# Eighty-one groups of twelve equal matmuls behind the last product of a two-layer decoder

## The chip, the cores and the metric

The kernel runs on one core of one Trainium2 chip. The metric is the device time of one execution in microseconds (us), the median of the runs. The core's engines are TensorE (PE in the profile; its weight loads are shown apart as PEld), VectorE (DVE), ScalarE (ACT), GpSimd (POOL) and SyncE (SP, which issues transfers). They run side by side and wait for each other by semaphores. SBUF is the core's working memory with 128 partitions; PSUM is where TensorE writes its results, in banks of 512 four-byte columns.

## The reference

A decoder trunk of two layers on 512 tokens with 1024 features, all in four-byte floating point. Each layer does this:

```python
h = rmsnorm(x, g_mix)
z = h @ w_in
aq, ak, av, rq, rk, rv, rg, ga, gb = jnp.split(z, SPLIT_POINTS, axis=-1)
...
ya = sliding_window_sink_attention(aq, ak, av, sinks) @ w_a
...
r = chunkwise_retention(rq, rk, rv)
...
yb = r.astype(x.dtype) @ w_b
mixed = jax.nn.sigmoid(ga) * ya + jax.nn.sigmoid(gb) * yb
x = x + mixed @ w_out
h2 = rmsnorm(x, g_mlp)
x = x + jnp.square(jax.nn.relu(h2 @ w_up)) @ w_down
```

The output is the RMS norm of x after the second layer.

## The kernel before

**Precision.** TensorE multiplies in a reduced four-byte form, fp32r. To keep more of the precision, every operand is split into a high and a low part, both fp32r (`hi` and `lo` for weights, `xh` and `xl` for the scaled inputs, pairs of tiles `r` for intermediate results), and a product is made of three matmuls: high by high, high by low, low by high. The helper `products` (lines 390 to 397) issues them, and nearly all of the kernel's TensorE time stands on its three lines 395, 396 and 397.

**Operands of a matmul.** A matmul has a stationary operand of 128 columns, which a weight load (LDWEIGHTS) puts into the array, and a moving operand of up to 512 columns that streams past it. The result goes to PSUM. In a profile row `mm<-xh,hi 128*128 128x512` the first name behind the arrow is the moving operand, the second the stationary one, and 128x512 is the result, so 512 columns are moved. The program has one load for each matmul.

**Stages.** In each layer `layer_body` multiplies by the input projection chunk by chunk, with attention and retention worked in between, then by the value, mixing and output projections, then runs the feed-forward part in eight blocks of 512 hidden features (`pair` and `down`). Larger products use Strassen-like sums of quarters, with 256 columns moved at a time. Everywhere in these products both operands are read at unit step. Their starts are whole multiples of 128 elements from the tile's start, except that the weights of `pair` and of the output projection start 16 elements (`LINE`) further in.

**The end of the kernel.** The last block of the second layer is multiplied plainly by `down_plain`: eight results of 128 tokens by 512 features, each the sum of four times three matmuls with 512 columns. The last of them is made in two halves of 256 columns. Behind each, VectorE adds it to the residual, ScalarE sums the squares, and when a token block's second half is done the block is scaled by its inverse RMS (lines 1680 to 1685) and stored by two transfers (lines 1683 and 1686). TensorE has nothing to do after the last half.

**Order.** A scheduler sets the order of each engine's instructions from the code and from `tc.issue_after`, which keeps what is issued under it behind a given instruction. `latest[0]` holds the last product matmul issued. PSUM tiles come from two pools, `ps_mm` with five banks and `ps_aux` with three; a pool hands out its banks in turn, and who takes a bank waits until its earlier use is over.

**Tiles that the change reads.** `xh` and `xl` hold the scaled layer input, 128 partitions by eight chunks of 512 elements, 4096 elements in a row for each partition. They were last written ahead of the second layer's feed-forward part.

Of the kernel before, what the change touches and what calls it, by code (L numbers as in the profile page):

```python
# [17 lines left out]
P = 128  # L18
T = 512
# [26 lines left out]
N_PAIR = 14  # L46
UNIT = 1024
LINE = 16
ASIDE = ("pair", "wo")
WARM = 8  # L50
PACE = 0.8
# [61 lines left out]
def view(slot):  # L113
    return slot[0][:, slot[1], :]
# [3 lines left out]
def decoder(ctx, tc, xT, x_first, w_in, w_rv, w_a, w_b, w_wo, w_up, w_pair, w_down, w_end, tables, decay, band, g_last, out):  # L118
# [203 lines left out]
    def split_until(n):  # L322
        while state["split"] < min(n, len(order)):
# [7 lines left out]
            elif name == "block":  # L331
                add_block(i)
            raw = raws[i]
            aside = LINE if name in ASIDE else 0
            hi, lo = (
                wpool.tile([P, UNIT + 4 * LINE], F32R, tag=n, name=n, bufs=SPLIT + 1)[:, aside : aside + UNIT]
                for n in ("hi", "lo")
# [281 lines left out]
    def layer_body(layer):  # L619
# [759 lines left out]
        first_hi, first_lo = (view(t).rearrange("p (a t) -> p a t", t=H) for t in u_one)  # L1379
        columns = small.tile([P, 2 * NB + LINE], F32, tag="columns", name="columns", bufs=1)  # L1380
        factor, negative = (columns[:, i * NB : (i + 1) * NB] for i in range(2))
# [399 lines left out]
        layer_body(layer)  # L1781

def _by_chunk(w, cols):

    return w[:, cols].reshape(-1, P, len(cols)).transpose(1, 0, 2)
# [158 lines left out]
```

## Time and profile before

| what | value |
|---|---|
| time, median of 2 runs | 1454.8 us (1454.45 to 1455.14) |
| the profiled execution's own time | 1457.31 us |
| its span, first to last instruction | 1455.2 us |
| mean granted TensorE clock | 0.999 of full speed |
| matmuls and weight loads | 8041 and 8041 |

The span is that of the profiled execution. The profile gives the busy time of each engine, and for matmuls that needs care: they are pipelined, so that the next one starts long before the former has ended, and the ends are modelled. What a matmul costs in a stream is the distance from its start to the next one's start, which the timeline shows.

### The profile page before, as it was taken

The page shows a single profiled execution, that of the slowest core. Times are in us where ns is not written, and L with a number is a line of the kernel's source. Part 1 is how long each engine was busy: PE and PEld are TensorE (multiplying, and loading weights), DVE is VectorE, ACT ScalarE, POOL GpSimd, SP SyncE. Part 2 cuts the span into 40 slices and gives each one's busy share as a digit, 9 for nine tenths or more (in the row PEclk, how much of TensorE's full clock was granted, in tenths as well). Part 3 has the DMA queues.
Part 4 walks back from the last instruction along what each step waited for, and adds up shares of the span by engine and source line. Part 5 has one row for each costly group of instructions (what it writes and reads, how often), then busy time and mean ns, then how long its engine had stood idle before and what let it go on. Part 6 is the DMA issues. An engine that isn't in the chain of part 4 may idle for free.

```text
span 1455.2 us, 22150 instructions
## 1 busy us (share of the span) xinstructions
PE 1443.0 (99%) x8041; PEld 1258.8 (87%) x8041; DVE 1167.0 (80%) x1762; ACT 969.2 (67%) x1592; POOL 222.6 (15%) x329
## 2 busy tenths in 40 slices
PE   9999999999999999999999999999999999999998
PEld 7888888888988999999888888888889799999997
DVE  6978876866998888888778788687778988787885
ACT  6657555543687777777756575565437877777775
POOL 0011012112101111112201110112120011111120
PEclk9999999999999999999999999999999999999999
DMA  7598359799745677666955983797875477777664
GB/s 258 177 290 225 105 165 303 237 247 248 232 124 196 191 200 186 175 182 179 310 177 170 295 222 108 215 293 223 221 214 175 138 202 199 195 193 197 177 188 149
DMA packets 96428, 297.57 MB, mean 204 GB/s; under 512 B 11328, under 2 KB 11456, under 8 KB 90432
## 3 DMA queue, kind: packets, MB, share of 16 engines
q0 software_dynamic: 35936, 125.58, 37.2%
q1 hardware_dynamic: 59664, 169.27, 33.5%
q8 instruction: 63, 1.03, 0.3%
q10 hardware_dynamic: 720, 1.31, 0.2%
q14 instruction: 45, 0.37, 0.1%
HBM read 256.54 MB, written 115.87 MB: 256 GB/s over the span
## 4 chain that ended last, share of the span: by engine, by line
PE 94%; DMA 2%; ACT 2%; DVE 1%; issue 1%; SPq 0%; DVEq 0%; ACTq 0%
PE mm L395 23%; PE mm L396 23%; PE mm L397 22%; PE wo L1301 5%; PE b L395 2%; PE b L396 2%; PE b L397 2%; PE rv L396 2%; PE rv L395 2%; PE rv L397 2%; PE mm L410 2%; DMA raw<-w_pair_in 1%; PE score L778 1%; PE pT L743 1%; PE r L397 1%; PE r L396 1%
## 5 line engine op out<-in xcount | busy, mean ns | idle before, releaser
L343 ACT ACTIVATE hi<-raw 128x1024 fp32r<-128x1024 f32 (+1 forms) x387 | 394.3, 1021 | 257.5 <-PE mm L396 137.1
L344 DVE TENSOR_TENSOR lo<-raw,hi 128x1024 fp32r<-128x1024 f32 (+1 forms) x388 | 452.3, 1173 | 105.8 <-ACT hi L343 104.4
L395 PE MATMUL mm<-xh,hi 128*128 128x512 f32 (+1 forms) x976 | 343.1, 355 | 1.6 <-ACT xh L418 0.9
L396 PE MATMUL mm<-xl,hi 128*128 128x512 f32 (+1 forms) x976 | 343.6, 355 | 0.0
L397 PE MATMUL mm<-xh,lo 128*128 128x512 f32 (+1 forms) x976 | 339.5, 354 | 0.0
L395 PEld LDWEIGHTS mm<-xh,hi 128*128 128x128 f32 x976 | 183.9, 189 | 27.6 <-ACT xh L418 1.6
L396 PEld LDWEIGHTS mm<-xl,hi 128*128 128x128 f32 x976 | 185.0, 190 | 24.2
L397 PEld LDWEIGHTS mm<-xh,lo 128*128 128x128 f32 x976 | 182.7, 188 | 23.6
L397 PE MATMUL mm<-r,lo 128*128 128x256 f32 (+1 forms) x608 | 187.9, 309 | 0.0
L396 PE MATMUL mm<-r,hi 128*128 128x256 f32 (+1 forms) x608 | 187.9, 309 | 0.0
L395 PE MATMUL mm<-r,hi 128*128 128x256 f32 (+1 forms) x608 | 185.6, 309 | 0.5 <-ACT mm L1476 0.5
L395 PEld LDWEIGHTS mm<-r,hi 128*128 128x128 f32 x608 | 114.7, 189 | 8.5 <-ACT mm L1476 0.7
L396 PEld LDWEIGHTS mm<-r,hi 128*128 128x128 f32 x608 | 115.2, 189 | 7.8
L397 PEld LDWEIGHTS mm<-r,lo 128*128 128x128 f32 x608 | 114.1, 188 | 6.2
L1624 POOL DMA_DIRECT2D y<-eu x56 | 62.3, 1351 | 370.8 <-DVE eu L1609 370.2
L396 PE MATMUL mm<-lo,r 128*128 128x512 f32 (+1 forms) x276 | 104.6, 388 | 0.0
L397 PE MATMUL mm<-hi,r 128*128 128x512 f32 (+1 forms) x276 | 101.3, 387 | 0.0
L395 PE MATMUL mm<-hi,r 128*128 128x512 f32 (+1 forms) x276 | 98.4, 390 | 0.9 <-ACT eu L1619 0.6
L395 PE MATMUL b<-hi,r 128*128 128x512 f32 x180 | 70.5, 392 | 1.6 <-DVE eu L1609 1.2
L396 PE MATMUL b<-lo,r 128*128 128x512 f32 x180 | 70.3, 390 | 0.0
L1301 PE MATMUL wo<-r,hi 128*128 128x256 f32 x384 | 68.0, 281 | 0.0
L397 PE MATMUL b<-hi,r 128*128 128x512 f32 x180 | 67.9, 390 | 0.0
(323 smaller groups left out, 2679.5 us busy)
## 6 DMA issues: line engine op xcount, KB each, us to landing
raw<-w_in_in SPq DMA_DIRECT2D x73, 512.0 KB, 5.9
sums_down<-w_down_in POOLq DMA_DIRECT2D x30, 1024.0 KB, 11.6
sums_up<-w_pair_in POOLq DMA_DIRECT2D x56, 512.0 KB, 10.5
raw<-w_down_in SPq DMA_DIRECT2D x45, 512.0 KB, 7.8
raw<-w_pair_in SPq DMA_DIRECT2D x84, 256.0 KB, 3.7
y<-y POOLq DMA_DIRECT2D x63, 256.0 KB, 9.2
y<-eu POOLq DMA_DIRECT2D x61, 256.0 KB, 8.0
raw<-sums_down SPq DMA_DIRECT2D x30, 512.0 KB, 7.3
```

Source lines behind the costliest of these rows:

```text
L343: state["high"] = nc.scalar.activation(hi[:, at], raw[:, at], AF.Copy).ins
L344: nc.vector.tensor_tensor(lo[:, at], raw[:, at], f32(hi[:, at]), ALU.subtract)
L395: nc.tensor.matmul(ps, ah, bh, start=start and i == 0, stop=False, **more)
L396: nc.tensor.matmul(ps, ah, bl, start=False, stop=False, **more)
L397: latest[0] = nc.tensor.matmul(ps, al, bh, start=False, stop=stop and i == n - 1, **more).ins
L410: latest[0] = nc.tensor.matmul(ps, w[:, cols(j, c)], moving[k][low], start=first, stop=bool(final)).ins
L743: nc.tensor.transpose(pt[:, i * P : (i + 1) * P], sm[:, at : at + P], ident)
L778: nc.tensor.matmul(ps[:, g * w : (g + 1) * w], q_s[g][:, c, at], part[:, keys], start=i == 0, stop=i == 1)
L1301: latest[0] = nc.tensor.matmul(o, w[:, cols], v, start=start and first and n % 2 == 0 and w is hi and v is vh, stop=final and w is lo, ski ...
L1624: nc.gpsimd.dma_start(y[:, 2 * j + m, i * T : (i + 1) * T], t, **how)
```

## The change

A function `paces` is called once behind the two layers. It takes `xh` as a long row `mv` of 4096 elements for the moving operand and `xl` as a row `st` for the stationary one. Its inner `run` takes a bank of `ps_aux` and issues the same matmul twelve times into it, under `issue_after(latest[0])`. Each is complete in itself (`start` and `stop`), and nothing reads the result. The calls differ in width (512 or 256 columns) and in where the operands lie:

- the stationary operand at unit step, from 0, 8, ..., 120 elements on, and from 2, 4 and 12;
- the moving operand from 4 and 8 elements on;
- the stationary operand with a step of 2, 4, 8, 16 or 30 elements, from 0 and 16 on;
- the moving operand in pieces of 16 elements out of every 32, with the stationary operand at step 1, 8 or 16;
- the moving operand with a step of 2;
- the moving operand and the result both backwards, with the stationary operand from 0, 16, 32 and 48 on.

```diff
+REPEAT = 12
...
+    def paces():
+        mv, st = (t.rearrange("p k t -> p (k t)") for t in (xh, xl))
+
+        def run(n, a, b, backwards=False):
+            ps = bank(ps_aux, "pace")
+            o = ps[:, n - 1 :: -1] if backwards else ps[:, :n]
+            with tc.issue_after(latest[0]):
+                for _ in range(REPEAT):
+                    latest[0] = nc.tensor.matmul(o, a, b, start=True, stop=True).ins
+
+        def lines(at, n):
+            return mv[:, at : at + 2 * n].rearrange("p (a b) -> p a b", b=2 * LINE)[:, :, :LINE]
+
+        def spread(at, step):
+            return st[:, at : at + P * step : step] if step > 1 else st[:, at : at + P]
+
+        for at in range(0, P, 8):
+            for n in (T, P * 2):
+                run(n, spread(at, 1), mv[:, :n])
+        for at in (2, 4, 12):
+            run(T, spread(at, 1), mv[:, :T])
+        for at in (4, 8):
+            for back in (0, 16):
+                run(T, spread(back, 1), mv[:, at : at + T])
+        for step in (2, 4, 8, 16, 30):
+            for at in (0, 16):
+                for n in (T, P * 2):
+                    run(n, spread(at, step), mv[:, :n])
+        for step in (1, 8, 16):
+            for at in (0, 16):
+                for n in (T, P * 2):
+                    run(n, spread(at, step), lines(0, n))
+        for n in (T, P * 2):
+            run(n, spread(0, 1), mv[:, : 2 * n : 2])
+        for at in (0, 16, 32, 48):
+            for n in (T, P * 2):
+                run(n, spread(at, 1), mv[:, n - 1 :: -1], True)
+
+    paces()
```

Since the new constant stands at the file's head, the lines of the kernel are numbered one higher behind it (395 is 396 after the change). On TensorE the program before ends with the last half of the last product; `hi` is the moving weight tile, `r_85` the stationary one.

```order
L397 MATMUL mm<-hi,r_85 128x256
L395 MATMUL mm<-hi,r_85 128x256
L396 MATMUL mm<-lo,r_85 128x256
L397 MATMUL mm<-hi,r_85 128x256
L1941 UNCONDITIONAL_BRANCH
```

After the change the same place on TensorE reads as follows, with the waits in brackets; `PE_49` is TensorE's own count of finished work.

```order
L398 MATMUL mm<-hi,r_85 128x256
L1793 MATMUL pace<-xh,xl 128x512 x12
L1793 MATMUL pace<-xh,xl 128x256 x12
L1793 MATMUL pace<-xh,xl 128x512 x12
L1793 MATMUL pace<-xh,xl 128x256 [waits PE_49]
L1793 MATMUL pace<-xh,xl 128x256 x11
L1793 MATMUL pace<-xh,xl 128x512 [waits PE_49]
```

The groups stand behind everything else on TensorE, in the order of the code, and from the fourth on the first matmul of a group waits for the group that had the same bank. The rows of all other engines are the same as before.

## The prediction

> **What bounds the kernel now.** I read the page's busy shares first, then its chain of work, because the added work stands on one engine and the question is whether that engine sets the end.
>
> ```profile
> span 1455.2 us, 22150 instructions
> ...
> PE 1443.0 (99%) x8041; PEld 1258.8 (87%) x8041; DVE 1167.0 (80%) x1762; ACT 969.2 (67%) x1592; POOL 222.6 (15%) x329
> ...
> PEclk9999999999999999999999999999999999999999
> ...
> PE 94%; DMA 2%; ACT 2%; DVE 1%; issue 1%; SPq 0%; DVEq 0%; ACTq 0%
> ```
>
> TensorE (PE) has a matmul running in 99% of the span, 94% of the chain that ended last is PE, and the granted clock is full in every slice. PE and PEld have the same count, 8041: each matmul has a weight load of its own. So whatever is added to PE costs its full time, except where PE has already stopped. That exception is the tail, read from the timeline.
>
> ```profile
> 1434.99 0.40 PE L395 MATMUL mm<-hi,r 128*128 128x512 f32 x1
> ...
> 1445.66 0.39 PE L397 MATMUL mm<-hi,r 128*128 128x512 f32 x1
> 1445.88 0.28 PE L395 MATMUL mm<-hi,r 128*128 128x256 f32 x1
> ...
> 1448.52 0.28 PE L396 MATMUL mm<-lo,r 128*128 128x256 f32 x1
> 1448.64 0.28 PE L397 MATMUL mm<-hi,r 128*128 128x256 f32 x1
> ...
> 1450.61 0.72 ACT L1685 ACTIVATE x<-x,sq 128x512 f32<-128x512 f32 x1 [0.23 <-DVE sq L1681]
> ...
> 1451.36 0.37 ACTq L1686 DMA_DIRECT2D y_out<-x  x1
> ```
>
> The first column is the start. PE starts its last matmul at 1448.64. What follows is the last block's normalization on VectorE (DVE) and ScalarE (ACT) and its store, and the span ends at 1455.2, 6.5 us after PE's next free place (1448.64 + 0.12 = 1448.76). That is all the cover that the added matmuls can have.
>
> **The price of one added matmul.** The durations are of no use here, since matmuls overlap: what a stream costs is the distance from start to start. Between 1434.99 and 1445.88 stand 48 matmuls with 512 columns: 10.89 / 48 = 0.227 us each. From 1445.88 to 1448.64 are 23 steps of matmuls with 256 columns: 2.76 / 23 = 0.120 each. Two longer or odder stretches bound the second figure.
>
> ```profile
> 1379.83 0.28 PE L397 MATMUL mm<-r,lo 128*128 128x256 f32 x1
> ...
> 1384.43 0.28 PE L397 MATMUL mm<-xh,lo 128*128 128x256 f32 x1
> ...
> 1385.13 0.28 PE L396 MATMUL mm<-r,hi 128*128 128x256 f32 x1
> ...
> 1386.27 0.28 PE L397 MATMUL mm<-r,lo 128*128 128x256 f32 x1
> ```
>
> The first pair is 39 steps in 4.60 us, 0.118 each; the second 10 steps in 1.14, 0.114 each. I take 0.118, the longest stretch, with 0.114 and 0.120 as its ends.
>
> [...]
>
> What does a weight load cost by itself? Where matmuls are one column wide, the loads are all that is left.
>
> ```profile
> 24.96 0.95 PE L566 MATMUL ssq<-ones,acc 128*128 128x1 f32 x8
> 25.77 0.72 PE L397 MATMUL mm<-xh,lo 128*128 128x512 f32 x2
> ...
> L395 PEld LDWEIGHTS mm<-xh,hi 128*128 128x128 f32 x976 | 183.9, 189 | 27.6 <-ACT xh L418 1.6 <-DVE rot L640 1.1 <-ACT eu L1478 0.5
> ```
>
> Eight such matmuls take 25.77 - 24.96 = 0.81 us; the first load was done ahead, so seven loads take at most 0.81 / 7 = 0.115 each. The load's own row shows 0.189 us, but most of that lies beside the matmul ahead of it. So with 256 columns a step is 0.118 and the load nearly fills it (0.115); with 512 there is about 0.11 of slack. A slower load shows at once in the groups with 256 columns, and in those with 512 only when it about doubles.
>
> **The change, part by part.** Counting the calls gives 81 groups: 32 in the first loop, 3, 4, 20 with a stepped stationary operand, 12 with a moving operand in pieces, 2 with a moving step of two, 8 backwards. 44 have 512 columns and 37 have 256: 44 x 12 = 528 and 37 x 12 = 444, together 972 matmuls with 972 loads.
>
> - At the pace of the rows: 528 x 0.227 = 119.9 us and 444 x 0.118 = 52.4 us, 172.3 in all.
> - Stationary places of 0 to 120 elements and moving places of 4 and 8, at unit step (39 groups): nothing but the place is new, and the kernel's own matmuls already differ in place (weights 16 elements in, in the pair loop, against none elsewhere); the spread that these show is 0.114 to 0.120. I add nothing.
> - Stepped stationary operands, 28 groups (20 and 8 of the 12 in pieces), 14 of each width: no row shows one. From below a load in steps costs nothing more, since the load's 128 elements are the same number. From above, none of a load lies beside a matmul: 0.189 more for each of 336, 63.5 us. I take nothing, the value of the nearest row, a load of the same size at unit step.
> - Moving operand in pieces of 16 out of 32 elements, in steps of two, or backwards with the result also backwards (22 groups): no row shows these either. From below nothing; from above each column takes twice as long, as the 4-byte transposes show.
>
> ```profile
> 83.28 0.60 PE L743 MATMUL pT<-ident,sm 128*128 128x128 f32 x4
> ```
>
>   Four transposes of 128 columns: (0.60 - 0.27) / 3 = 0.11 us each, 0.86 ns a column, where the difference of the two widths, (0.227 - 0.118) / 256, is 0.43 ns. For 22 groups, 11 of each width, that is 132 x (0.227 + 0.118) = 45.5 us. I take nothing: the count of columns is unchanged, which is what the matmul rows scale with.
> - Waits: from the fourth group on, the first matmul of a group waits for PE's own count, that the group three earlier is done (three banks). Two groups of twelve lie between, at least 24 x 0.114 = 2.7 us, so the count is long there when it is asked for. The table of PE's waits bears it out: its longest row is 1.2 us, and none names PE itself, though products in it already wait that way. Behind a waiting matmul only later groups are queued. Cost: nothing; if it were not hidden, a drain of 0.28 at 78 groups is 22 us, inside the range.
> - Other engines: nothing is added or moved. The operands xh and xl were written long before and nothing is read from the results.
>
> ```profile
> PE b L395 <- DVE eu L1609: 1.2, 1, 1.2
> ...
> PE wo L1301 <- ACT xh L418: 0.2, 1, 0.2
> ...
> DMA to landing us min/median/max: 2.0/2.4/2.8
> ```
>
> The end: the last store is issued at 1451.36 and lands 2.0 to 2.8 later, so closing the program takes 1.0 to 1.8 us of the span (1455.2 less 1454.2 or 1453.4); I take 1.2. Now the close waits for PE. The first added matmul starts at 1448.76, the last at 1448.76 + 172.3 - 0.1 = 1621.0, it ends 0.28 later, and with 1.2 the span is 1622.4, that is 167.2 more than 1455.2. The whole tail of 1448.76 to 1455.2 disappears under the new stream. The profiled execution took 1457.31 us, 2.5 above the median of 1454.8, so for itself it would come to 1624.5; on the median it is 1454.8 + 167.2 = 1622.
>
> **The rivals.**
>
> - Half-pace loads. A load whose elements lie 16 bytes or more apart takes twice as long, 0.23 us. Steps of 4, 8, 16 and 30 elements are in 12 groups of each width: 144 x (0.230 - 0.118) + 144 x (0.230 - 0.227) = 16.6 us, giving 1639. For it speaks how tight the load is at 256 columns; against it, that no row shows any load slower than another in SBUF. [...]
> - Loads far slower, or stealing from the moving stream in both widths: half to all of the 63.5 us above, 1654 to 1686. That each load already costs its matmul something (0.118 for 256 columns at 0.43 ns is 0.008 above 0.110) speaks for some of it.
> - Backwards or stepped moving operands at half pace: the 8 backward groups and the 2 with step two are 60 x (0.227 + 0.118) = 20.7 us, giving 1643; the two alone, 4.1.
> - Loads that cost nothing, since the same weights are loaded twelve times: 0.43 ns a column gives 0.218 and, at the load's floor, 0.113: 528 x 0.218 + 444 x 0.113 = 165.3, giving 1615. [...]
> - Not slower by 2%: equal matmuls in a row are folded into one. 81 x 0.18 = 14.6 us, less the cover of 6.5, is 8 more: 1463. It decides from a stream below 6.5 + 29 us on. Against it: the warm-up at line 375 issues eight equal matmuls and the trace has all eight, with their loads.
>
> ```profile
> L375 PE MATMUL warm<-ones 128*128 128x512 f32 x8 | 3.8, 649 | 1.1 <-DVE ones L370 1.1
> L375 PEld LDWEIGHTS warm<-ones 128*128 128x128 f32 x8 | 2.5, 325 | 1.6 <-DVE ones L370 1.1
> ```
>
> **How the numbers follow.** Pace as in the rows, 1616 to 1628 around 1622: 0.40. Half-pace loads, around 1639: 0.26. Backward or stepped moving, 1626 to 1645: 0.12. Far slower loads, 1654 and more: 0.15. Free loads, 1615: 0.04. Folded: 0.02. A remainder of 0.01 that no case gives. The range of 1612 to 1660 takes in the first three and the free loads, 0.82, and cuts most of the slow loads. A measurement of this kernel tells about 2%, 29 us, from no change: slower 0.97, within 2% 0.02, faster 0.01.
>
> **What would show it.** In the profile after: 972 more on PE and on PEld, at line 1793, starting at about 1448.8; each group's twelve starts 0.227 or 0.114 to 0.120 apart; no row of waits of PE on PE; the granted clock still full; ScalarE's and VectorE's last work still ending near 1451.4. Half-pace loads would show as groups with steps of 4 and more and 256 columns near 0.23, with step 2 and the 512 ones unchanged. Slower moving operands would show in the last ten groups at both widths. The prediction is wrong if the stepped, cut or backward groups, 42 of the 81, run at a pace of their own; the 39 at unit step are its safe part.

## The result and the profile after

The changed kernel takes 1646.82 us, the median of 2 runs (1646.69 to 1646.94), against 1454.8 us (1454.45 to 1455.14) before: a ratio of 1.132, 95% interval 1.1271 to 1.1369. That is slower by 192.0 us. The forecast was 1622.0 with a range of 1612 to 1660, so the sign and the range held, and the centre lies 24.8 us too low.

These are the lines of after that answer to those shown of before: span, busy time of the engines, granted clock, and the chain that ended last by engine; the last row is from the view of that chain in order of time.

```profile
span 1644.7 us, 24094 instructions
...
PE 1637.6 (100%) x9013; PEld 1435.6 (87%) x9013; DVE 1167.4 (71%) x1762; ACT 968.6 (59%) x1592; POOL 223.0 (14%) x329
...
PEclk9999999999999999999999999999999999999999
...
PE 96%; ACT 2%; DMA 1%; DVE 1%; issue 0%; SPq 0%; DVEq 0%; ACTq 0%
...
1446.33 197.41 PE pace L1793 x972
```

9013 - 8041 = 972 matmuls and as many loads: all were issued and all were run, none folded into another. The other engines' busy times are those of before to within 0.6 us, and the clock stayed full in every slice. The last row (start, length, what it is) is the end of the chain of work: the added stream alone fills 197.41 us with nothing else in it, and only the 1.0 us of closing the program follows. The table of PE's waits has no row in which PE waits for PE.

So the stream itself was longer than the 172.3 us forecast, and the question is which groups. The next view gives the stream by stretches of time, each cut a little inside its first and last group. Its columns are the stretch and its length, the busy time and number of matmuls (PE) and of loads (PEld), the granted clock, the share of DMA, and GB/s.

```profile
1446.40:1532.60 86.20, 86.20 (x467) 74.16 (x466) 1.00 0.02 7
1533.10:1541.10 8.00, 8.00 (x46) 7.10 (x45) 1.00 0.00 0
1541.60:1586.90 45.30, 45.30 (x192) 45.30 (x191) 1.00 0.00 1
1587.40:1595.60 8.20, 8.20 (x47) 6.98 (x46) 1.00 0.00 0
1596.10:1618.20 22.10, 22.10 (x96) 22.10 (x95) 1.00 0.00 1
1618.70:1626.40 7.70, 7.70 (x24) 4.59 (x23) 1.00 0.00 0
1626.90:1643.40 16.50, 16.50 (x95) 14.34 (x94) 1.00 0.00 1
```

In the order of the code these are: unit places, stationary step 2, stationary steps 4 to 30, moving pieces with a unit stationary operand, the same with a stepped one, moving step two, and backwards. PEld gives a first hint. In five stretches loads are busy for 60% to 90% of the time; in the third and the fifth they are busy for all of it (45.30 of 45.30, 22.10 of 22.10). That alone proves little, since plain groups with 256 columns also keep the loads busy throughout (1.30 of 1.30 us in the second group). But plain groups with 512 columns don't (2.07 of 2.50 in the first), and here those do too, which points at the loads. The sixth is the opposite: 24 matmuls fill 7.70 us while their loads take only 4.59, which points at the moving operand.

Taken from the first matmul of each stretch to the first of the next, and set against the forecast's prices of 0.227 and 0.118 us:

| stretch | matmuls | us | forecast | more |
|---|---|---|---|---|
| unit places | 468 | 86.74 | 85.3 | 1.4 |
| stationary step 2 | 48 | 8.43 | 8.28 | 0.15 |
| stationary steps 4, 8, 16, 30 | 192 | 45.78 | 33.1 | 12.7 |
| moving pieces, unit stationary | 48 | 8.70 | 8.28 | 0.4 |
| moving pieces, stationary step 8 or 16 | 96 | 22.58 | 16.56 | 6.0 |
| moving step two | 24 | 8.22 | 4.14 | 4.1 |
| backwards | 96 | 16.96 | 16.56 | 0.4 |

Together 25.2 us: 18.7 from the two stretches with stationary steps of 4 and more, 4.1 from the moving step of two, 2.4 from all else. Within the third stretch, the groups with 256 columns run at 0.233 (step 4), 0.240 to 0.243 (step 8), 0.221 to 0.223 (step 16) and 0.243 to 0.244 us (step 30) from start to start, where the forecast had 0.118; those with 512 columns at 0.235 to 0.248. (This leaves out each group's first step, where it meets the group ahead: about 0.35 with 512 columns and 0.12 with 256, together two loads at this pace.) In the sixth, the widths take 0.455 and 0.230, twice the forecast.

The rest of the account is small. The products ended 2.6 us earlier in this execution than in the one of before (first added matmul at 1446.17, forecast 1448.76), and the program closed 1.25 us after the last matmul's start where 0.28 + 1.2 was forecast. 167.2 + 25.2 - 2.6 - 0.2 = 189.6, and the spans differ by 1644.7 - 1455.2 = 189.5.

### The profile page after: what moved, and what is told of

It is laid out like the page before. It is cut to its first block, busy times and chain, and to the rows that moved or that the text cites. A ratio compares the mean times of both kernels' runs of the same rounds, so it can differ in the third digit from the quotient of the medians.

```text
span 1644.7 us, 24094 instructions
## 1 busy us (share of the span) xinstructions
PE 1637.6 (100%) x9013; PEld 1435.6 (87%) x9013; DVE 1167.4 (71%) x1762; ACT 968.6 (59%) x1592; POOL 223.0 (14%) x329
## 4 chain that ended last, share of the span: by engine, by line
PE 96%; ACT 2%; DMA 1%; DVE 1%; issue 0%; SPq 0%; DVEq 0%; ACTq 0%
PE mm L396 20%; PE mm L398 20%; PE mm L397 20%; PE pace L1793 12%; PE wo L1302 5%; PE b L396 2%; PE b L397 2%; PE b L398 2%; PE rv L398 2%; PE rv L397 2%; PE rv L396 2%; PE mm L411 1%; PE score L779 1%; PE pT L744 1%; PE r L398 1%; PE r L397 1%
## 5 line engine op out<-in xcount | busy, mean ns | idle before, releaser
L1793 PE MATMUL pace<-xh,xl 128*128 128x512 f32 (+1 forms) x972 | 197.6, 366 | 0.0
L1793 PEld LDWEIGHTS pace<-xh,xl 128*128 128x128 f32 x972 | 177.7, 229 | 19.8 <-issue 3.0
L396 PE MATMUL b<-hi,r 128*128 128x512 f32 x180 | 70.5, 393 | 1.6 <-DVE eu L1610 1.2
```

The source lines that it names most:

```text
L396: nc.tensor.matmul(ps, ah, bh, start=start and i == 0, stop=False, **more)
L1793: latest[0] = nc.tensor.matmul(o, a, b, start=True, stop=True).ins
```

## The experiments

All but the last keep the changed kernel up to its last product and replace only what `paces` issues there, so the output is computed as before; the added results are unread in all of them. From the second experiment on a measured group has twenty-four matmuls, so that the distance from one row to the next, divided by 24, is the pace; "steady" leaves out a group's first steps. The paces in the five experiments with such groups come from one execution each. The plain group with 512 columns, which three of them have, came out at a steady 0.2272 each time.

### Steps of four and more, and the moving step of two, back at unit step

```diff
-        for step in (2, 4, 8, 16, 30):
+        for step in (2, 1, 1, 1, 1):
...
-        for step in (1, 8, 16):
+        for step in (1, 1, 1):
...
-            run(n, spread(0, 1), mv[:, : 2 * n : 2])
+            run(n, spread(0, 1), mv[:, :n])
```

> The changed kernel with 26 of its 81 groups put back to unit step: the 24 whose stationary operand has a step of 4, 8, 16 or 30, and the 2 whose moving operand has a step of 2. The 972 matmuls stay. Theory A (a step that leaves fewer than two of the read elements on a 16-byte line halves a weight load, and a step of two halves the moving stream; all else runs at the pace of unit step): in the changed kernel the 24 groups took 45.8 + 22.6 us and the 2 took 8.2; at unit step they should take 144 x (0.233 + 0.119) = 50.7 and 12 x (0.228 + 0.119) = 4.2, so 21.7 us less, 1625 against 1646.8. Theory B (the excess over 172 us belongs to the backward groups, the waits for a bank, or the end of the program): at most 10 us less, 1637 or more.

Measured: 1625.9 us (1624.45 to 1628.56), a ratio to before of 1.117, interval 1.1151 to 1.1188. Its page begins:

```profile
span 1622.4 us, 24094 instructions
...
PE 1615.7 (100%) x9013; PEld 1409.3 (87%) x9013; DVE 1167.7 (72%) x1762; ACT 969.5 (60%) x1592; POOL 223.1 (14%) x329
```

The same number of instructions, and the span is 22.3 us shorter than with the change as it is. Group by group, the 26 that were made plain take 54.8 us here and 76.6 in the changed kernel: 21.8 less, where theory A expected 21.7. (It is 12.39 in the stationary steps with a plain moving operand, 5.33 in those with a moving operand in pieces and 4.05 in the moving step of two.) The step of the operands is therefore the cause, and not the place in the program or the number of matmuls. The stationary step of 2, the moving pieces and the backward groups stayed as they were. What remains, 1625.9, is within 4 us of the forecast, which had taken steps to be free.

### What a stepped load costs

Twelve groups with a moving operand at unit step, 256 columns wide and then 32, and stationary steps of 1 to 31; `same` repeats one column 128 times.

```diff
+        run("one", P * 2, every(st, P, 1), half)
+        run("two", P * 2, every(st, P, 2), half)
+        run("three", P * 2, every(st, P, 3), half)
+        run("four", P * 2, every(st, P, 4), half)
...
+        run("oneslim", 32, every(st, P, 1), slim)
...
+        run("fourslim", 32, every(st, P, 4), slim)
+        run("sameslim", 32, same(st, P), slim)
```

> In place of the 81 groups, 12 groups of 24 with other steps of the stationary operand: 7 beside 256 moving columns, 5 beside 32, where only the load is left. Theory A (the load's read costs about 1.75 ns for each 16-byte line that it touches, and never less than 0.112 us): step 1, 2 and one column repeated 0.112 to 0.120 us a matmul; step 3 touches 96 lines, 0.17; steps 4, 5 and 31 touch 128 lines each, all 0.22 to 0.24. Beside 32 columns: 0.112, 0.112, 0.17, 0.225 for steps 1, 2, 3, 4 and 0.11 for the repeated column. Theory B (the distance to the element before decides: under 16 bytes free, from 16 on double): step 3 (12 bytes) stays at 0.118, 4, 5 and 31 as in A. Theory C (the step lengthens the load through conflicts with the moving stream alone): beside 32 columns step 4 stays near 0.12.

The timeline of PE, with one row for each group (start, length, instruction, number):

```profile
1448.65 3.04 PE L1792 MATMUL one<-xh,xl 128*128 128x256 f32 x24
1451.52 3.04 PE L1792 MATMUL two<-xh,xl 128*128 128x256 f32 x24
1454.40 4.32 PE L1792 MATMUL three<-xh,xl 128*128 128x256 f32 x24
1458.56 5.76 PE L1792 MATMUL four<-xh,xl 128*128 128x256 f32 x24
1464.16 5.65 PE L1792 MATMUL five<-xh,xl 128*128 128x256 f32 x24
...
1478.06 2.75 PE L1792 MATMUL oneslim<-xh,xl 128*128 128x32 f32 x24
1480.65 5.13 PE L1792 MATMUL twoslim<-xh,xl 128*128 128x32 f32 x24
...
1490.74 5.74 PE L1792 MATMUL fourslim<-xh,xl 128*128 128x32 f32 x24
1496.33 5.28 PE L1792 MATMUL sameslim<-xh,xl 128*128 128x32 f32 x24
```

Step 1 and step 2 run at 2.87 / 24 = 0.120, step 3 at 4.16 / 24 = 0.173, step 4 at 5.60 / 24 = 0.233, and steps 5 and 31 at 0.229 and 0.233. This is not a jump at a distance of 16 bytes, which would have left step 3 with its 12 bytes free. The price goes with a count: in groups of four elements from the tile's start, 16 bytes each and called lines here, the 128 elements touch 64 at step 2, 96 at step 3 and 128 from step 4 on, and 0.173 / 96 and 0.233 / 128 are both 1.8 ns a line. Among loads of 128 lines the price still varies: in the changed kernel from 0.221 at step 16 to 0.244 at step 30, or 1.7 to 1.9 ns a line, and no run shows why. At step 2 the 64 lines (0.116 at that price) just disappear behind what a load takes anyhow: with 32 columns and step 1, where the moving operand is out of the way, a steady step is 0.112.

Put by elements: with two to a line a matmul beside 256 columns takes no longer than with four (0.120 at steps 1 and 2), and with one it takes 1.94 times as long (0.233 against 0.120).

The slim groups hold a trap, which the granted clock shows (the columns now have DVE, ACT and POOL behind PEld, none busy; the clock stands third from the end).

```profile
1478.06:1480.65 2.59, 2.59 (x26) 2.59 (x25) 0.00 (x0) 0.00 (x0) 0.00 (x0) 1.00 0.03 6
1490.74:1496.30 5.56, 5.56 (x25) 5.56 (x26) 0.00 (x0) 0.00 (x0) 0.00 (x0) 0.50 0.00 0
```

From the group `twoslim` on the clock is 0.50, and `twoslim`'s steady 0.213 is the floor of a load at half clock and not the price of a step of 2: the repeated column, a single line, takes 0.213 as well. Yet `fourslim` is at 0.233 as `four` was at full clock. So the price of 128 lines doesn't scale with TensorE's clock. It is no conflict with the moving operand either, since with 32 columns there is next to none.

### What a stepped moving operand costs

Twelve groups with 512 columns and a stationary operand at unit step: moving steps of 1 to 7, pieces of two or four elements out of eight at two starts, and one column repeated.

```diff
+        run("two", T, plain, every(mv, T, 2))
+        run("three", T, plain, every(mv, T, 3))
...
+        run("pairs", T, plain, pieces(mv, T, 2, 8))
...
+        run("quads", T, plain, pieces(mv, T, 4, 8))
+        run("quadsacross", T, plain, pieces(mv, T, 4, 8, 2))
+        run("samecolumn", T, plain, same(mv, T))
...
+        run("weightsame", T, same(st, P), every(mv, T, 1))
```

> In place of the 81 groups, 12 groups of 24 with 512 moving columns in other patterns. Theory A (the moving read costs about 1.7 ns for each change of 16-byte line): unit step 128 lines, 0.227 us; step 2, 256 lines, 0.45; step 3, 384 lines, 0.67; steps 4 and 7, 512 lines, 0.88 to 0.92; pairs of every eight elements that share a line, 256 lines, 0.45; the same pairs three elements further on, so that each lies across two lines, 512 lines, 0.9; quads of every eight on one line 0.23, two elements further on 0.45; one column repeated 0.216 or less. Theory B (any step but one halves the rate, whatever the lines): steps 2, 3, 4 and 7 all 0.45, pairs and quads between 0.23 and 0.45 and the same wherever they start. [...]

The same view of this kernel:

```profile
1447.95 5.63 PE L1792 MATMUL one<-xh,xl 128*128 128x512 f32 x24
1453.41 11.04 PE L1792 MATMUL two<-xh,xl 128*128 128x512 f32 x24
1464.27 10.98 PE L1792 MATMUL three<-xh,xl 128*128 128x512 f32 x24
1475.07 11.26 PE L1792 MATMUL four<-xh,xl 128*128 128x512 f32 x24
1486.14 10.69 PE L1792 MATMUL seven<-xh,xl 128*128 128x512 f32 x24
1496.65 11.27 PE L1792 MATMUL pairs<-xh,xl 128*128 128x512 f32 x24
1507.74 11.22 PE L1792 MATMUL pairsacross<-xh,xl 128*128 128x512 f32 x24
1518.78 5.73 PE L1792 MATMUL quads<-xh,xl 128*128 128x512 f32 x24
1524.34 11.09 PE L1792 MATMUL quadsacross<-xh,xl 128*128 128x512 f32 x24
1535.26 5.43 PE L1792 MATMUL samecolumn<-xh,xl 128*128 128x512 f32 x24
1540.52 5.41 PE L1792 MATMUL bothsame<-xh,xl 128*128 128x512 f32 x24
```

Step 2 takes 0.453 and steps 3, 4 and 7 take 0.450, 0.461 and 0.438: the price doubles at once and then grows no more, about 0.88 ns a column. Four elements together run at full pace (0.231) when they fill one line and at half (0.455) when they start two elements further on and lie over two lines; pairs are at half pace whether both elements lie on one line (0.462) or on two (0.460). Both theories fell. The one that let the price grow with every further line was wrong from step 3 on and for the pairs on two lines, and the other was wrong on the groups of four.

Two elements to a line, at which a load costs no more (0.120), are not enough for the moving operand: at full clock two are half pace (0.453 at step 2), and full pace was seen only with four (0.231).

The last groups bear on a side question, why a plain matmul takes 0.227 and not 512 x 0.43 = 0.218. With one moving column repeated it takes 0.219 (5.26 / 24), with one weight column repeated 0.232: about 8 ns of the 0.227 go with reading different moving columns, and reading different weight columns adds nothing. Each matmul here still has its load, so whether a load beside the stream matters is not shown.

### The law on other shapes

Thirteen groups to try one formula: a moving operand takes 1.75 ns or more for each line that it touches, never less than 0.43 nor more than 0.88 ns a column; a load takes 1.75 or more for each line, never less than 0.112.

```diff
+        run("byone", T, plain, every(mv, T, 1, 1))
...
+        run("sixofeight", 3 * P, plain, pieces(mv, 3 * P, 6, 8))
+        run("sixteens", T, plain, pieces(mv, T, 16, 32))
+        run("sixteensbytwo", T, plain, pieces(mv, T, 16, 32, 2))
+        run("eightsbytwo", T, plain, pieces(mv, T, 8, 16, 2))
+        run("halvestwo", P * 2, plain, every(mv, P * 2, 2))
...
+        run("quarterthree", P, every(st, P, 3), mv[:, :P])
```

> In place of the 81 groups, 13 groups of 24. Nine with other moving patterns, four with a load of step 1 to 4 beside 128 moving columns, in place of the 32 beside which the clock fell to half. Moving: the runs so far give 0.43 ns a column where four neighbours share a 16-byte line and 0.88 where not, however far apart. Theory A (each line takes at least 1.75 ns and each column at most 0.88): unit step started one, two or three elements in costs a line more, 0.227 to 0.235; six of every eight elements, 384 columns, 0.225; pieces of sixteen 0.24 where they start on a line and 160 lines, 0.28, where they start two elements in; pieces of eight two elements in, 192 lines, 0.34; 256 columns at step 2, 0.225. Theory B (the whole instruction falls to 0.88 ns a column as soon as any group of four is not on one line): 0.45 for unit step started one, two or three in, 0.34 for six of eight, 0.45 for pieces started two in. Loads beside 128 columns: if the full clock holds, 0.112, 0.112, 0.17, 0.23 for steps 1 to 4 (a price of the load itself); if the slowness of steps came from the 256 columns that stream beside it, steps 3 and 4 fall well below 0.17 and 0.23.

```profile
1470.63 5.62 PE L1792 MATMUL sixofeight<-xh,xl 128*128 128x384 f32 x24
1476.07 5.93 PE L1792 MATMUL sixteens<-xh,xl 128*128 128x512 f32 x24
1481.84 7.22 PE L1792 MATMUL sixteensbytwo<-xh,xl 128*128 128x512 f32 x24
1488.89 8.15 PE L1792 MATMUL eightsbytwo<-xh,xl 128*128 128x512 f32 x24
1496.87 5.68 PE L1792 MATMUL halvestwo<-xh,xl 128*128 128x256 f32 x24
1502.37 2.81 PE L1792 MATMUL quarterone<-xh,xl 128*128 128x128 f32 x24
```

Steady paces: pieces of 16 on whole lines 0.240, two elements off a line 0.295, pieces of eight two off 0.330, six of eight 0.227 for only 384 columns. Only the parts of a moving operand that fall on half-filled lines slow down; a single odd piece does not put the whole instruction to half pace, as the rival had it. Starting 1, 2 or 3 elements off a line at unit step costs 0.237, 0.233 and 0.229 against 0.227. The moving paces lie within some 7% of the formula; the largest miss is the pieces of 16 on whole lines, 128 lines or 0.224 by the formula.

The last four groups put loads of step 1 to 4 beside 128 columns. They run at a steady 0.112, 0.118, 0.173 and 0.233, the third as long as the clock is full. So the price belongs to the load and not to the 256 columns that streamed beside it.

### Do walking, alternating or adding matter?

The forecast's two prices at 256 columns, 0.114 and 0.120, came from different places of the kernel, and the change's unit places gave 0.113 at starts of 16 and 80 and up to 0.120 elsewhere. Sixteen groups vary what the kernel does and the added groups don't: another weight each time, two moving tiles in turn, adding into one bank.

```diff
+            walk("fixed" + place, P * 2, lambda i: half[0], lambda i: weights(st, 0, at))
+            walk("adding" + place, P * 2, lambda i: half[0], lambda i: weights(st, 0, at), True)
+            walk("walking" + place, P * 2, lambda i: half[0], lambda i: weights(st, i % 8, at))
+            walk("turns" + place, P * 2, lambda i: half[i % 2], lambda i: weights(st, 0, at))
...
```

> In place of the 81 groups, 16 groups of 24 at unit step: 12 with 256 columns, six with the stationary operand 16 elements in and six with it even with the moving one, and 4 with 512 columns. In each six: operands that stay, the same adding up in PSUM, a stationary operand that walks by 128 columns, a moving operand that changes between two tiles, both changing as in the kernel's products, and that adding up. Theory A (the place within 64 elements alone sets the pace): all six that are 16 in run at 0.113, all six that are even at 0.120, and the kernel's 0.118 in its products comes from somewhere else. Theory B (what changes between matmuls matters too): the groups that walk or change go to 0.117 or 0.118 as the kernel's do, and one of walking, changing or adding up is what does it. With 512 columns: 0.227 to 0.233, the same question.

```profile
1448.14 2.99 PE L1805 MATMUL fixedin<-xh,xl 128*128 128x256 f32 x24
1450.96 2.99 PE L1805 MATMUL addingin<-xh,xl 128*128 128x256 f32 x24
```

A miss for both theories. All six groups with weights 16 elements in ran at 0.118 (2.82 / 24 in the first) and all six even ones at 0.120, whatever was varied; the four with 512 columns at a steady 0.2267 to 0.2272. None of the variations matters, but the 0.113 that the same place had shown in the changed kernel was not there. The place alone doesn't decide it.

### Two steady paces

What differed was what ran ahead. Fourteen times twelve matmuls with 512 columns, then a single different matmul or none, then twenty-four with 256 columns and weights 16 in.

```diff
+        def state(name, *kicks):
+            run_of(T, "wide", 12, 0)
+            for i, (n, w) in enumerate(kicks):
+                run_of(n, "kick" + name, 1, w)
+            run_of(H2, name, 24, 16)
...
+        state("none")
+        state("slim", (16, 16))
...
+        state("halfeven", (H2, 0))
...
```

> In place of the 81 groups, 14 times: 12 matmuls with 512 columns, then none, one or two other matmuls, then 24 with 256 columns and the stationary operand 16 elements in. In the kernel's own products such matmuls run at 0.1178 where steady ones with 512 columns lie ahead, and at 0.1135 behind a pause or behind ones with 512 columns that ran at 0.233 to 0.236; the changed kernel's groups at 16 and 80 ran at 0.1133 behind a group at 0.233. Theory A (two steady phases of load against stream, and what lies ahead picks one): without anything between, 0.1178; behind one or two 512-column matmuls with the stationary operand 16 in, or behind a stalled one, 0.1135 for at least one of the kinds. Theory B (place of the operands in higher address bits decides, not history): all 14 at 0.1178.

```profile
1451.85 2.99 PE L1810 MATMUL none<-xh,xl 128*128 128x256 f32 x24
1454.67 2.91 PE L1810 MATMUL wide<-xh,xl 128*128 128x512 f32 x12
1457.42 0.17 PE L1810 MATMUL kickslim<-xh,xl 128*128 128x16 f32 x1
1457.45 2.98 PE L1810 MATMUL slim<-xh,xl 128*128 128x256 f32 x24
...
1503.22 0.28 PE L1810 MATMUL kickhalfeven<-xh,xl 128*128 128x256 f32 x1
1503.33 2.88 PE L1810 MATMUL halfeven<-xh,xl 128*128 128x256 f32 x24
1506.05 2.92 PE L1810 MATMUL wide<-xh,xl 128*128 128x512 f32 x12
```

With nothing between, the twenty-four run at 2.82 / 24 = 0.118 (1451.85 to 1454.67). Behind one matmul of the same width with even weights they run at 2.72 / 24 = 0.113 (1503.33 to 1506.05). Behind a slim kick the first step takes 0.201, the next two 0.122 and 0.116, and the others 0.113; over only twenty-four the kick gains nothing (2.85 us from 1457.42 to 1460.27, against 2.82). In all, seven of the twelve kinds of kick led to 0.113 (also one of 64, 128 or 512 columns with weights 16 in, and one of 256 with weights 32 in or with a step), and five left 0.118: two slim ones, a slim one or one of 128 columns with even weights, two of 512 columns, and one of 256 with weights 8 in. Equal instructions thus have two steady paces, 0.113 and 0.118, and what runs just ahead picks which, for the whole group of twenty-four. Why there are two, and which kicks tip the stream, remains open.

### The kernel before, with a kick ahead of its 256-column streams

The last experiment asks whether this is worth anything in the kernel itself. It is the kernel before, without the change, plus small matmuls with 16 columns into a bank that the next product overwrites; the trace has 16 of them.

```diff
+    def kick(ps, w):
+        nc.tensor.matmul(ps[:, :LINE], w, xh[:, 0, :LINE], start=True, stop=True)
...
+                    if ps is a and start and u == 0:
+                        kick(ps[0], hi[:, :P])
...
+            if not which:
+                kick(e, part[0][:, 4 * P : 5 * P])
```

> The kernel before, without the 81 groups, with 15 small matmuls of 16 columns added: one ahead of each layer's output projection and one in the first pair of each feed-forward block, where long runs of matmuls with 256 columns begin behind ones with 512. The small result is overwritten by the product that follows. Theory A (two steady phases, and a small matmul ahead tips the run into the faster one, as it did behind the steady 512s in the run with kicks): some 2 x 287 and 1700 matmuls go from 0.1178 to 0.1134, 10.0 us less, for 15 x 0.12 to 0.13 = 1.9 more: 8 us faster, a ratio near 0.9945. Theory B (the phase does not last, because every wait or change of bank in the real products sets it anew): 2 us slower, 1.001. Theory C (the phase lasts but TensorE then waits for the split weights of ScalarE and VectorE): between 0 and 4 us faster.

Measured: 1449.1 us (1447.79 to 1450.82) against 1456.61 (1454.54 to 1457.96) for the kernel before, measured beside it: a ratio of 0.9948, interval 0.9935 to 0.9962. That is 7.5 us or 0.5%, small but clear of no change, and what theory A forecast (0.9945). PE's timeline of the kernel before at one block of `pair`: the row ahead of a stream of 132 matmuls with 256 columns, the stream's first row and the row that ends it:

```profile
489.48 0.39 PE L397 MATMUL b<-hi,r 128*128 128x512 f32 x1
489.71 0.28 PE L395 MATMUL mm<-r,hi 128*128 128x256 f32 x1
...
505.25 0.63 PE L395 MATMUL mm<-hi,r 128*128 128x512 f32 x2
```

The same with the kick:

```profile
489.23 0.39 PE L397 MATMUL b<-hi,r 128*128 128x512 f32 x1
489.45 0.17 PE L402 MATMUL mm<-xh,hi 128*128 128x16 f32 x1
489.48 0.37 PE L395 MATMUL mm<-r,hi 128*128 128x256 f32 x1
...
504.54 0.63 PE L395 MATMUL mm<-hi,r 128*128 128x512 f32 x2
```

Before, 505.25 - 489.71 = 15.54 us; with the kick, its own start included, 504.54 - 489.45 = 15.09. Over the whole execution, 2426 of the 3215 steps at 256 columns are below 0.116 us with the kicks and 272 of 3215 without them. Together these steps take 374.31 us against 381.95, which is 7.64 less, while those with 512 columns take 0.7 more: the gain lies in the pace of the 256-column streams. Besides the kicks, some short stretches of the same products run in another order, which the runs don't take apart. At the first block a kick landed inside a running stream, and the stream behind it stayed at 0.118.

## Why the prediction was right, and where it failed

- **TensorE is the bound, and the addition costs its full time: right.** The chain ends with 197.41 us of nothing but the added stream, and the old tail disappeared under it.
- **0.227 and 0.118 for plain matmuls: right.** With the steps of four and more and the moving step of two made plain, the kernel took 1625.9, against 1622 forecast. The even groups of the experiments gave 0.227 and 0.120, and unit places cost 1.4 us in 86.74 more than the rows had it.
- **Waits of PE on its own count cost nothing: right.** No row of PE's waits names PE.
- **Backwards adds nothing: right,** 0.4 us in 17. **Moving pieces of 16: nearly right,** 0.4 us in 8.7; with 512 columns they run at 0.237 to 0.247 and not 0.227.
- **Stepped stationary operands, "I take nothing, the value of the nearest row": this step failed,** and the two stretches that have them hold 18.7 of the 25.2 us (17.7 by the run that put them back to unit step). The nearest row showed 128 elements at unit step, which touch 32 lines of 16 bytes; steps of 4 and more touch 128, and a load paid 1.8 ns for each (0.233 / 128) where that exceeded the 0.112 of a dense one beside 32 columns. The forecast had noticed how tight this was (a load of at most 0.115 in a step of 0.118) and still chose the lower end of the range, because no row showed a slow load. But no row had a stepped load at all, so the rows spoke for neither. The first rival priced it: half-pace loads, 16.6 us, 1639. It was right that such a load takes about twice as long (0.233 against 0.120 us a step) and short by 2.1 us, mostly since the groups with 512 columns grew from 0.227 to between 0.235 and 0.248 and were priced at 0.230. Its condition of 16 bytes or more left out that step 3, at 12 bytes, already costs about half as much more (0.173).
- **Moving step of two, "I take nothing: the count of columns is unchanged": this failed too,** with 4.1 us. The third rival had exactly this figure for the two groups alone, from the transposes at 0.86 ns a column; the experiments found 0.88. That the two agree is luck as far as the runs show: the kernel's transposes read both operands at unit step, so their rate can't come from half-used lines.
- **Free loads (1615), far slower loads (1654 and more) and folding (1463) did not come.** Nothing came near the 63.5 us bound of a load with nothing beside it. For 1612, the lower end of the range, the 972 matmuls would have had to take 162 us, 10 less than forecast; no run shows such a pace, and at the lowest steady ones that the runs show for plain matmuls, 0.2267 and 0.113, they would take 169.9 (an estimate, 528 x 0.2267 + 444 x 0.113).

The two failed steps that the rivals priced, 16.6 + 4.1, would have put the forecast at 1643.

The range held because it was drawn wide enough to take in these rivals, not because the centre's mechanism was right. By its own sign of being wrong, that some of the 42 stepped, cut or backward groups run at a pace of their own, the prediction plainly failed in 26 of them. Two small readings were off without consequence: 0.81 / 7 is 0.116 and not 0.115, and the cover of the tail is 6.4 us and not 6.5.

## What to carry to other kernels

In these runs a matmul's price was set by the columns only as long as both operands lay densely: count the 16-byte lines that each touches. In this kernel's four-byte form a load cost nothing more with two elements to a line (0.120 us a step with 256 columns) and about twice as much with one (0.233), and a moving operand of 512 columns was at full pace only with four elements on one line (0.231) and at half pace with two or fewer (0.438 to 0.462). Where no row of a profile shows a kind of access, "the nearest row" says nothing about it, and a rival that names the mechanism and can be priced deserves the centre of the forecast. When measuring a pace, look at the granted clock in the same window and at what ran just ahead.

## What the runs showed of the hardware that was not expected

- Two steady paces for the same stream, 0.113 and 0.118 us for 256 columns, chosen by what runs just ahead of it: seven of the twelve kinds of kick tipped it into the faster one. Used on the kernel before, it brought 0.5%.
- The granted clock fell to 0.50 behind 2.59 us of matmuls with 32 columns, although PE had no gap; it fell too where 128 columns stood beside loads of step 3, in the experiment on other shapes: 0.89 on the mean from 1508.00 to 1512.00 us and 0.50 from 1512.30 to 1517.50. Beside loads of step 1 and 2 it had stayed at 1.00. The price of a load with one element to a line, 0.233, was the same at both clocks.
- The pace at unit step depended on the start of the stationary operand and repeated every 64 elements to within 0.0001 us: with 512 columns 0.229 at 0 and 64, 0.230 at 48 and 112, and 0.233 to 0.234 at the other multiples of 8. How much of this is place and how much is what ran ahead was not taken apart.
